# The mLSTM of a hybrid encoder block issued in one written order, its decay rows loaded and masked apart, and waits kept per tile

## The chip, the core and the metric

The kernel runs on one core of a Trainium2 chip. The core has four compute engines with their own instruction streams (TensorE, called PE in the profile; VectorE, DVE; ScalarE, ACT; GpSimd, POOL) and SyncE (SP), whose stream here only issues DMA transfers. ScalarE issues transfers too. Each engine takes its instructions strictly in the order of its stream; engines wait for one another by semaphores. The metric is the device time of one execution in microseconds (us). The kernel before took 2719.76 us in the median of three runs, 2715.68 to 2721.2.

## The reference, cut to what matters

One layer on x of 2048 positions by 1024 channels, all float32: a pre-norm, one input projection, two groups of heads side by side, an output projection with residual, and a squared-ReLU MLP with residual. Group A is four heads of a bidirectional mLSTM, in chunks of 128 positions (16 per head); group B is a Hyena long convolution by FFT. The part that the change rewrites is group A:

```python
def mlstm_chunkwise(q, k, v, log_i, log_f):          # one direction, heads of 128 channels
    bcum = jnp.cumsum(log_f.reshape(B, H, NC, L), axis=-1); g = bcum[..., -1]
    a = g[..., None] - bcum + li
    def step(carry, xs):                             # the state, from chunk to chunk
        m_new = jnp.maximum(g_c + m, jnp.max(a_c, axis=-1))
        decay = jnp.exp(g_c + m - m_new); w = jnp.exp(a_c - m_new[..., None])
        C_new = decay[..., None, None] * C + jnp.einsum('bhl,bhld,bhle->bhde', w, k_c, v_c)
        n_new = decay[..., None] * n + jnp.einsum('bhl,bhld->bhd', w, k_c)
    dmat = jnp.where(causal, bcum[..., :, None] - bcum[..., None, :] + li[..., None, :], -jnp.inf)
    m_t = jnp.maximum(bcum + m_s[..., None], jnp.max(dmat, axis=-1))
    s_qk = jnp.einsum('bhctd,bhcsd->bhcts', qc, kc) * jnp.exp(dmat - m_t[..., None])
    inter_scale = jnp.exp(bcum + m_s[..., None] - m_t)
    num = einsum(s_qk, vc) + inter_scale[..., None] * einsum(qc, C_s)
    den = s_qk.sum(-1) + inter_scale * einsum(qc, n_s)
    return num / jnp.maximum(jnp.abs(den), jnp.exp(-m_t))[..., None]
h_m = (h_fwd + h_bwd) * o_gate                       # then an RMS norm per head
```

## The kernel before, in words

The program is one stream of stages: pre-norm and input projection (with the Hyena filters beside it), the Hyena convolutions with the last pieces of the projection woven in, the mLSTM, the output projection, the MLP. All matrices stay in float32; each large product is three passes of TensorE (lines 159 to 161) over split operands.

`mlstm()` (L881) does the four heads in a software pipeline over n = 0 to 68. The names, which the rows use:

- `turned(h, g)`, L939: four transposes `ptk` of a key group into one PSUM tile `kt`, of which there is one, and from it the weighted keys `kw`, four ScalarE instructions for the forward direction (L950) and one of VectorE for the backward one (L952). Head h+1 is turned in steps 6 to 9 of head h.
- `state_step(h, step)`, L954: four products `pv` (two directions) and two VectorE updates `st` (L971) that carry the states from chunk to chunk. Head h+1's fifteen steps run two per n from step 8 of head h; head 0's fifteen all stand ahead of n = 0.
- `weights(h, g)`, L974: the load of the decay rows `mb` of four chunks, broadcast to 128 partitions, and two GpSimd masks (L980, L981).
- `scores(h, ch)`, L984: the products `pS` of a chunk, two ScalarE exponentials on `mb` (L993), and for every fourth chunk one VectorE product `pm` of scores and weights (L996).
- `values(h, ch)`, L999, five steps later: the products `ps` (query by state) and `pa` (weights by v); `scaled` (two ScalarE instructions `nm`, L1015), `sums` (VectorE, L1018), and for every fourth chunk the quotients `den` (VectorE) with `nm` times `den` and `ht` (GpSimd, L1028, L1030), stored by ScalarE's queue (`ym<-ht`). These later pieces are kept in a list and issued at the end of step n by `issue(n)`.

PSUM tiles of `pv`, `ps` and `pa` come from one pool of five (`mps`). Loads of the next heads' k, v and q stand in a table `LOADS` by step.

The order: the Hyena part runs inside `tc.manual_schedule()`, in which every engine issues what the code emits, in that order. `mlstm()` does not; there a scheduler orders the emitted work by its own estimate of when each piece is ready. Tile pools have a rule for reusing bytes of pools that were released: by default a first user waits for all users of those earlier pools; with `reuse_waits="tile"` it waits only for users of the earlier tiles on its own bytes. Three pools had that before.

Of the kernel before, what the change touches and what calls it, by code (L numbers as in the profile page):

```python
# [147 lines left out]
class Builder:  # L148
# [95 lines left out]
    def build(self):  # L244
        tc, nc = self.tc, self.nc
        with ExitStack() as c:
            cp = c.enter_context(tc.tile_pool(name="cp", bufs=1))
# [24 lines left out]
            with ExitStack() as c2:  # L272
                self.pw = pj.enter_context(tc.tile_pool(name="pwk", bufs=2, reuse_waits="tile"))
                self.pp = pj.enter_context(tc.tile_pool(name="pps", bufs=4, space=PSUM))
# [7 lines left out]
            gp = c.enter_context(tc.tile_pool(name="gp", bufs=1, side="right"))  # L282
# [6 lines left out]
            for i, n in enumerate(("mlstm_norm_w", "hyena_norm_w")):  # L289
# [3 lines left out]
                   hy.enter_context(tc.tile_pool(name="hps", bufs=3, space=PSUM, side="right")))  # L293
# [7 lines left out]
            op = self.op = late.enter_context(tc.tile_pool(name="opre", bufs=1, side="right"))  # L301
# [3 lines left out]
            self.mtail = late.enter_context(tc.tile_pool(name="mtail", bufs=2, side="right"))  # L305
# [5 lines left out]
            self.h1p = c.enter_context(tc.tile_pool(name="h1p", bufs=2, space=PSUM))  # L311
            oc = ExitStack()
            self.hq = c.enter_context(tc.tile_pool(name="hmq", bufs=1))
# [6 lines left out]
            hp = c.enter_context(tc.tile_pool(name="hmp", bufs=1, side="right"))  # L320
            self.hm_pool.update({i: hp for i in (1, 2)})
            self.hm = {}
            self.cb = c.enter_context(tc.tile_pool(name="cb", bufs=1, side="right"))
# [10 lines left out]
    def long_conv(self, pools, hy, early):  # L334
# [16 lines left out]
    def filters(self, c, consts):  # L351
        tc = self.tc
        kp = c.enter_context(tc.tile_pool(name="kp", bufs=1, side="right"))
        wk = c.enter_context(tc.tile_pool(name="kwk", bufs=2, side="right"))
        ps = c.enter_context(tc.tile_pool(name="kps", bufs=2, space=PSUM, side="right"))
        yield from self.filter_net(kp, wk, ps, consts)
        yield from self.filter_spectra(kp, wk, ps, c.enter_context(tc.tile_pool(name="kmps", bufs=1, space=PSUM, side="right")))
# [523 lines left out]
    def mlstm(self):  # L881
# [3 lines left out]
        for ready in range(AHEAD // 4):  # L885
            self.weights(0, ready)
# [1065 lines left out]
```

## Time and profile before

| | us |
|---|---|
| median of three runs (2715.68 to 2721.2) | 2719.76 |
| the profiled execution | 2723.08 |
| its span, first to last instruction | 2721.3 |
| TensorE busy in it | 2602.7 (96%) |
| last projection piece to the first value step `ps` | 1026.4 to 1046.4 |
| value steps of head 0, 1, 2, 3 begin (n = 5, 16, 32, 48 of the pipeline) | 1046.4, 1069.1, 1107.2, 1144.1 |
| last `pa` of the mLSTM | 1174.1 |

The profile is one execution; times inside it are from its first instruction. Busy time is the union of an engine's instructions; the matmuls' ends are modelled, so the start of the next matmul says more of what one costs than its own length. The time in brackets behind a row is how long the engine stood idle before it, and after the arrow what ended that. "Granted clock" is the share of TensorE's full clock that the chip gave in that stretch; its two levels are 1.2 and 2.4 GHz.

### The profile page before, as it was taken

How to read it: one execution, taken by the hardware profiler on the slowest of the kernel's cores; microseconds unless marked ns; L12 is line 12 of the kernel's file. 1: busy time of each engine (PE TensorE's matmuls, PEld its weight loads, DVE VectorE, ACT ScalarE, POOL GpSimd, SP SyncE). 2: the span in 40 equal slices, each digit the busy share in tenths (PEclk: the TensorE clock that was granted, in tenths of full speed). 3: DMA queues.
4: the chain of work that ended last, by engine and by line, in shares of the span. 5: the costliest groups of instructions: out<-in, count | busy, mean ns of one | idle time of the engine just before them, and what ended most of it. 6: DMA issues, size and time to landing. Idle time of an engine off the chain costs nothing.

```text
span 2721.3 us, 35529 instructions
## 1 busy us (share of the span) xinstructions
PE 2602.7 (96%) x12293; PEld 2125.3 (78%) x12293; DVE 1527.1 (56%) x2453; ACT 1237.2 (45%) x2300; POOL 1220.3 (45%) x973
## 2 busy tenths in 40 slices
PE   6999999999999998889997999989999999999998
PEld 4778888777798887767775888868888888888876
DVE  5676653777547666656455444464444433544478
ACT  6355544555544446643334454454444333222244
POOL 1211114555235443446676877677772340311232
PEclk8999999999999999989998999989999999999999
DMA  6233346665676549556755444554446453444546
GB/s 172 61 87 113 112 124 215 191 190 175 215 234 185 181 154 297 152 158 222 231 177 200 171 138 166 181 185 150 148 163 254 164 181 108 121 146 159 186 161 218
DMA packets 288355, 465.76 MB, mean 171 GB/s; under 512 B 37542, under 2 KB 149414, under 8 KB 287152
## 3 DMA queue, kind: packets, MB, share of 16 engines
q1 hardware_dynamic: 227600, 324.85, 38.3%
q10 hardware_dynamic: 53264, 117.53, 11.4%
q0 software_dynamic: 7312, 21.11, 3.1%
q8 instruction: 98, 1.61, 0.3%
q14 instruction: 81, 0.66, 0.1%
HBM read 289.27 MB, written 174.13 MB: 170 GB/s over the span
## 4 chain that ended last, share of the span: by engine, by line
PE 40%; DVE 5%; POOL 3%; DMA 3%; ACT 2%; issue 2%; ACTq 0%; DVEq 0%; POOLq 0%; SPq 0%
PE pm L160 13%; PE pm L161 13%; PE pm L159 13%; DVE cb L169 1%; POOL xt L1255 1%; DVE hm L169 1%; ACT xo L1393 1%; DMA m<-ga 1%; DVE hm L1877 0%; DMA m<-in_w_mlp_out_dram 0%; POOL cb L169 0%; DMA hm<-ht 0%; DVE xo L1396 0%; POOL ht L1428 0%; DVE hm L1807 0%
## 5 line engine op out<-in xcount | busy, mean ns | idle before, releaser
L166 ACT CAST cb<-m 128x1024 fp32r<-128x1024 f32 (+1 forms) x346 | 281.2, 847 | 442.6 <-PE pm L159 387.5
L169 DVE TENSOR_TENSOR cb<-m,cb 128x1024 fp32r<-128x1024 f32 (+1 forms) x222 | 232.5, 1084 | 306.0 <-ACT cb L166 296.3
L160 PE MATMUL pm<-hm,cb 128*128 128x512 f32 x896 | 354.6, 396 | 18.4 <-DVE hm L169 13.2
L159 PE MATMUL pm<-hm,cb 128*128 128x512 f32 x896 | 354.1, 396 | 11.1 <-POOL cb L169 6.2
L161 PE MATMUL pm<-hm,cb 128*128 128x512 f32 x896 | 352.8, 394 | 0.0
L160 PE MATMUL pm<-cb 128*128 128x512 f32 x880 | 343.4, 390 | 7.8 <-DVE cb L169 7.8
L159 PE MATMUL pm<-cb 128*128 128x512 f32 x880 | 342.3, 389 | 1.0 <-DVE cb L169 1.0
L161 PE MATMUL pm<-cb 128*128 128x512 f32 x880 | 342.5, 389 | 0.0
L169 POOL TENSOR_TENSOR cb<-m,cb 128x1024 fp32r<-128x1024 f32 x124 | 270.7, 2196 | 71.6 <-ACT cb L166 71.6
L1689 DVE TENSOR_TENSOR m<-pm,m 128x512 f32<-128x512 f32 x224 | 154.2, 690 | 250.8 <-PE pm L161 224.7
L159 PE MATMUL pt<-hn,w 128*128 128x512 f32 x640 | 270.1, 422 | 1.7 <-ACT hn L486 1.6
L160 PE MATMUL pt<-hn,w 128*128 128x512 f32 x640 | 254.2, 397 | 0.3 <-DVE hn L487 0.2
L161 PE MATMUL pt<-hn,w 128*128 128x512 f32 x640 | 253.3, 396 | 0.0
L169 POOL TENSOR_TENSOR raw<-raw,hi 128x512 fp32r<-128x512 f32 x160 | 206.1, 1300 | 100.6 <-ACT hi L166 75.4
L160 PEld LDWEIGHTS pm<-hm,cb 128*128 128x128 f32 x896 | 170.5, 190 | 59.3 <-DVE hm L169 16.6
L159 PEld LDWEIGHTS pm<-hm,cb 128*128 128x128 f32 x896 | 170.6, 190 | 51.0 <-POOL cb L169 7.9
L160 PEld LDWEIGHTS pm<-cb 128*128 128x128 f32 x880 | 165.1, 188 | 45.9 <-DVE cb L169 11.8
L161 PEld LDWEIGHTS pm<-hm,cb 128*128 128x128 f32 x896 | 170.4, 190 | 36.1
L159 PEld LDWEIGHTS pm<-cb 128*128 128x128 f32 x880 | 165.1, 188 | 35.9 <-ACT junk L1862 1.4
L161 PEld LDWEIGHTS pm<-cb 128*128 128x128 f32 x880 | 165.2, 188 | 34.0
L1693 ACT ACTIVATE m<-m 128x512 f32<-128x512 f32 x128 | 80.5, 630 | 220.4 <-DVE m L1689 213.1
L635 POOL DMA_DIRECT2D vp<-vst x96 | 61.3, 642 | 232.0 <-ACT vst L631 230.9
(322 smaller groups left out, 5672.0 us busy)
## 6 DMA issues: line engine op xcount, KB each, us to landing
ga<-m ACTq DMA_DIRECT2D x96, 512.0 KB, 4.4
m<-ga SPq DMA_DIRECT2D x96, 512.0 KB, 3.8
d<-st ACTq DMA_DIRECT2D x64, 512.0 KB, 3.0
m<-in_w_mlp_in_dram SPq DMA_DIRECT2D x62, 512.0 KB
m<-in_w_mlp_out_dram SPq DMA_DIRECT2D x114, 256.0 KB, 4.0
raw<-d SPq DMA_DIRECT2D x96, 256.0 KB, 3.2
xt<-in_x_dram SPq DMA_DIRECT2D x32, 512.0 KB, 4.0
dk<-kst SPq DMA_DIRECT2D x32, 512.0 KB, 3.8
```

Of the source, the lines that this page charges most:

```text
L159: pe.matmul(ps, w[1], x[0], start=first, stop=False)
L160: pe.matmul(ps, w[0], x[1], start=False, stop=False)
L161: pe.matmul(ps, w[0], x[0], start=False, stop=last)
L166: self.act.copy(hi, src)
L169: (eng_lo or self.dve).tensor_tensor(lo, src, hi.bitcast(F32), ALU.subtract)
L635: pool.dma_start(dst[:, 8 * b + e:8 * b + 8:2, cc:cc + 128], st[64 * e:64 * e + 64])
L1255: eng.tensor_tensor(res[:, cs], tmp[e], res[:, cs], ALU.add)
L1393: act.activation(x1, xt, AF.Square, accum_out=ss1[:, h:h + 1])
L1689: dve.tensor_tensor(dst, a, b, ALU.add)
L1693: act.activation(g, g, AF.Relu)
```

## The change

1. Nearly all tile pools get `reuse_waits="tile"`.
2. `mlstm()` runs inside `tc.manual_schedule()`.
3. `weights` is cut in two: `weights_load` (the transfer) and `masked` (the two GpSimd masks), issued at different steps.
4. Head 0's fifteen state steps are spread over n = 0 to 4, three each.
5. `issue(n)` stands at the start of step n; `scaled` is emitted with `values` itself; `pm` is put off to the start of the next step.
6. `LOADS` begins with head 1's k at n = 1 (before: ahead of n = 0); head 1's v and q follow at 3 and 6; the rest is unchanged. The loads for the output projection (`loads_ahead`) go at n = 30 to 48, every second step, where they went at 50 to 59.
7. Head 0's weighted-key tiles are allocated before its k, v and q (`weighted_keys`), and the Hyena part allocates its first `st` and `ci` tiles first, which decides whose places the mLSTM's first tiles take.
8. The projection's last column group is stored by ScalarE's queue, no longer SyncE's (eight transfers `vo<-vst`).

The diff, cut to its core (the other pools change as the first one shown):

```diff
-            cp = c.enter_context(tc.tile_pool(name="cp", bufs=1))
+            cp = c.enter_context(tc.tile_pool(name="cp", bufs=1, reuse_waits="tile"))
...
-            self.mps = ms.enter_context(tc.tile_pool(name="mps", bufs=5, space=PSUM))
-            self.mlstm()
+            self.mps = ms.enter_context(tc.tile_pool(name="mps", bufs=5, space=PSUM, reuse_waits="tile"))
+            with tc.manual_schedule():
+                self.mlstm()
...
+        self.kw_first = {g: self.weighted_keys() for g in (0, 3, 1, 2)}
         self.head_loads(0, "kvq")
...
-                self.load(self.vo[128 * t - 128:128 * t + 128, N * g:N * g + n].rearrange("(u p) c -> p u c", p=128),
+                (self.store if g == order[-1] else self.load)(self.vo[128 * t - 128:128 * t + 128, N * g:N * g + n].rearrange("(u p) c -> p u c", p=128),
                           sts.pop((g, t // 2))[:, :, 0:n])
...
-        LAG, AHEAD = 5, 10
-        LOADS = {1: "v1", 5: "q1", 9: "k2", 14: "v2", 19: "q2", 32: "k3", 32 + LAG: "v3", 40: "q3"}
+        LAG = 5
+        LOADS = {1: "k1", 3: "v1", 6: "q1", 9: "k2", 14: "v2", 19: "q2", 32: "k3", 32 + LAG: "v3", 40: "q3"}
         self.later = []
-        for ready in range(AHEAD // 4):
-            self.weights(0, ready)
-        ready += 1
-        self.head_loads(1, "k")
-        for step in range(15):
-            self.state_step(0, step)
+        for g in range(4):
+            self.weights_load(0, g)
+        for g in range(2):
+            self.masked(0, g)
         for n in range(64 + LAG):
             self.now = n
             h, ch = divmod(n, 16)
-            while ready < 16 and ready <= (n + AHEAD) // 4:
-                self.weights(*divmod(ready, 4))
-                ready += 1
+            if n % 4 == 1 and 4 <= n // 4 + 3 < 16:
+                self.weights_load(*divmod(n // 4 + 3, 4))
+            self.issue(n)
             steps = [s for s in (2 * ch - 16, 2 * ch - 15) if h < 3 and 0 <= s < 15]
+            if n < 5:
+                for s in range(3 * n, 3 * n + 2):
+                    self.state_step(0, s)
+            if steps:
+                self.state_step(h + 1, steps[0])
             if n < 64:
-                if steps:
-                    self.state_step(h + 1, steps[0])
                 self.scores(h, ch)
                 if h < 3 and 6 <= ch < 10:
                     self.turned(h + 1, (0, 3, 1, 2)[ch - 6])
             if LAG <= n:
                 self.values(*divmod(n - LAG, 16))
+            if n < 5:
+                self.state_step(0, 3 * n + 2)
             if len(steps) > 1:
                 self.state_step(h + 1, steps[1])
             if n in LOADS:
                 self.head_loads(int(LOADS[n][1]), LOADS[n][0])
-            if 50 <= n < 60:
-                self.loads_ahead(n - 50)
+            if n % 4 == 3 and n // 4 + 2 < 16:
+                self.masked(*divmod(n // 4 + 2, 4))
+            if 30 <= n < 50 and n % 2 == 0:
+                self.loads_ahead((n - 30) // 2)
             if n in (61, 64, 64 + LAG - 1):
                 self.first_gate((61, 64, 64 + LAG - 1).index(n))
-            self.issue(n)
...
+    def weighted_keys(self):
+        return [self.mearly.tile([128, 4, 128], F32, tag=f"kw{d}", name=f"kw{d}", bufs=4) for d in range(2)]
...
-        if i == 3:
+        def weighted():
             pm = m["pm", g] = wk.tile([128, 2, 4, 128], F32, tag="pm", name="pm")
             self.dve.scalar_tensor_tensor(pm, pS.unsqueeze(1).to_broadcast([128, 2, 4, 128]), KSCALE, mb,
                                           ALU.mult, ALU.mult)
+        if i == 3:
+            self.later.append((self.now + 1, weighted))
...
-        work = [scaled, sums] + ([last, None, stored] if i == 3 else [])
+        scaled()
+        work = [None, sums] + ([last, None, stored] if i == 3 else [])
```

Outside of the mLSTM and the first pieces of the output projection the engines' orders stay as they were, but for those eight stores.

What stands on VectorE at the hand-over from the Hyena part (its last rows `z`) to the mLSTM, before and then now:

```order
L1155 TENSOR_TENSOR z<-z,pu 128x512
L952 TENSOR_TENSOR kw_10341<-ptk,qt 128x512
L952 TENSOR_TENSOR kw_10353<-ptk,qt 128x512
L971 SCALAR_TENSOR_TENSOR st<-st,decay,pv 128x129 x3
L952 TENSOR_TENSOR kw_10365<-ptk,qt 128x512
L971 SCALAR_TENSOR_TENSOR st<-st,decay,pv 128x129 x5
L952 TENSOR_TENSOR kw_10377<-ptk,qt 128x512
L971 SCALAR_TENSOR_TENSOR st<-st,decay,pv 128x129 x22
L996 SCALAR_TENSOR_TENSOR pm<-pS,mb 128x1024
```

```order
L1174 TENSOR_TENSOR z<-z,pu 128x512
L960 TENSOR_TENSOR kw_10287<-ptk,qt 128x512
L960 TENSOR_TENSOR kw_10289<-ptk,qt 128x512
L960 TENSOR_TENSOR kw_10291<-ptk,qt 128x512
L960 TENSOR_TENSOR kw_10293<-ptk,qt 128x512
L979 SCALAR_TENSOR_TENSOR st<-st,decay,pv 128x129 x24
L1007 SCALAR_TENSOR_TENSOR pm<-pS,mb 128x1024
L979 SCALAR_TENSOR_TENSOR st<-st,decay,pv 128x129 x6
```

The first eight state updates stood between the weighted keys; now all thirty stand behind the fourth, and the first `pm` has moved ahead of the last six.

What stands on ScalarE in the steps of head 0 and 1 without state work, exponentials `mb` and scaled numerators `nm`, before and now:

```order
L993 ACTIVATE mb<-mb,qt 128x128
L1015 ACTIVATE nm<-ps,qt 128x129 x2
L993 ACTIVATE mb<-mb,qt 128x128 x5
L1015 ACTIVATE nm<-ps,qt 128x129 x2
L993 ACTIVATE mb<-mb,qt 128x128 x6
L1015 ACTIVATE nm<-ps,qt 128x129 x2
```

```order
L1029 ACTIVATE nm<-ps,qt 128x129 x2
L1004 ACTIVATE mb<-mb,qt 128x128 x2
L1029 ACTIVATE nm<-ps,qt 128x129 x2
L1004 ACTIVATE mb<-mb,qt 128x128 x2
L1029 ACTIVATE nm<-ps,qt 128x129 x2
L234 DMA ym<-ht 128x4x128
L1004 ACTIVATE mb<-mb,qt 128x128 x2
L1029 ACTIVATE nm<-ps,qt 128x129 x2
```

Batches of up to six exponentials stood between two steps' numerators; now it is two and two throughout, with the store in its written place.

What stands on ScalarE at the end of the mLSTM, where the output projection's weights (`wo`) and its first operand (`y`, cast from PSUM `pty`) begin, before and now:

```order
L1015 ACTIVATE nm<-ps,qt 128x129 x6
L234 DMA ym<-ht 128x4x128
L1015 ACTIVATE nm<-ps,qt 128x129 x2
L1342 ACTIVATE wo_11960<-wf_10390,yw 128x1024
L166 CAST y_10396<-pty 128x512
```

```order
L1029 ACTIVATE nm<-ps,qt 128x129 x6
L1363 ACTIVATE wo_11963<-wf_10390,yw 128x1024
L234 DMA ym<-ht 128x4x128
L1029 ACTIVATE nm<-ps,qt 128x129 x2
L166 CAST y_10396<-pty 128x512
```

The first `wo` has moved ahead of the store and of the last numerators.

## Rows read from the trace of the kernel before

**Rows 1.** The page, busy time of TensorE: us, share of the span, instructions.

```profile
PE 2602.7 (96%) x12293; PEld 2125.3 (78%) x12293; DVE 1527.1 (56%) x2453; ACT 1237.2 (45%) x2300; POOL 1220.3 (45%) x973
```

**Rows 2.** The mLSTM cut into its stages (windows): start and end, length, then busy us (and instructions) of PE, PEld, DVE, ACT and POOL, the granted TensorE clock as a share of full speed, the DMA share and GB/s.

```profile
1026.40:1046.40 20.00, 14.46 (x97) 13.24 (x97) 10.82 (x35) 11.91 (x38) 3.73 (x7) 0.83 1.07 338
1046.40:1069.10 22.70, 21.04 (x156) 19.55 (x157) 18.90 (x53) 18.44 (x67) 6.60 (x8) 1.00 0.90 300
1069.10:1107.20 38.10, 31.41 (x213) 28.85 (x212) 24.97 (x67) 25.06 (x89) 19.09 (x21) 0.91 0.77 252
1107.20:1144.10 36.90, 30.85 (x205) 28.48 (x205) 22.73 (x66) 22.82 (x79) 16.10 (x19) 0.90 0.53 143
1144.10:1174.10 30.00, 27.07 (x158) 22.38 (x156) 18.92 (x46) 16.61 (x53) 18.62 (x14) 0.94 0.22 62
```

**Rows 3.** The timeline of TensorE inside the mLSTM, two places where nothing is waited for: start us, us from the first start to the last modelled end, line, operation, output from inputs, how many. What one piece costs the engine is the start of the next minus its own.

```profile
1038.08 0.39 PE L990 MATMUL pS<-q,k 128*128 128x128 f32 x2
1038.30 0.39 PE L966 MATMUL pv<-v,kw 128*128 128x129 f32 x2
1038.52 0.61 PE L990 MATMUL pS<-q,k 128*128 128x128 f32 x4
...
1048.02 0.60 PE L1008 MATMUL ps<-st,q 128*128 128x258 f32 x2
1048.46 0.61 PE L1010 MATMUL pa<-v,pm 128*128 128x129 f32 x4
1048.90 0.60 PE L945 MATMUL ptk<-eye,k 128*128 128x128 f32 x4
1049.34 0.60 PE L1008 MATMUL ps<-st,q 128*128 128x258 f32 x2
```

**Rows 4.** The hand-over from the Hyena part to the mLSTM, the timeline of SyncE's queue (one row) and of TensorE (three rows): the same columns, and in brackets the idle time before and what ended it.

```profile
1022.85 0.33 SPq L231 DMA_DIRECT2D k<-qk  x1
...
1027.87 0.63 PE L945 MATMUL ptk<-eye,k 128*128 128x128 f32 x4 [1.46 <-DMA k<-qk]
1030.57 1.12 PE L945 MATMUL ptk<-eye,k 128*128 128x128 f32 x4 [2.06 <-DVE kw L952]
...
1046.43 0.67 PE L1008 MATMUL ps<-st,q 128*128 128x258 f32 x2 [1.60 <-DVE st L971]
```

**Rows 5.** Groups of the stretch 1020 to 1195, ScalarE first and VectorE behind: count | busy us, mean ns of one | idle us before them and what ended it.

```profile
L993 ACT ACTIVATE mb<-mb,qt 128x128 f32<-128x128 f32 x128 | 42.4, 406 | 12.3 <-POOL mb L980 5.6 <-POOL ht L1030 3.6 <-DVE st L971 3.0
L1015 ACT ACTIVATE nm<-ps,qt 128x129 f32<-128x129 f32 x128 | 39.8, 373 | 33.4 <-PE ps L1008 17.0 <-POOL ht L1030 14.8 <-PE pa L1010 1.2
...
L971 DVE SCALAR_TENSOR_TENSOR st<-st,decay,pv 128x129 f32<-128x129 f32 x120 | 34.0, 342 | 13.3 <-PE pv L966 13.1
L1018 DVE TENSOR_TENSOR nm<-nm,pa 128x258 f32<-128x258 f32 x64 | 26.4, 419 | 25.4 <-ACT nm L1015 22.1 <-PE pS L990 2.2 <-PE pa L1010 0.2
L996 DVE SCALAR_TENSOR_TENSOR pm<-pS,mb 128x1024 f32<-128x1024 f32 x16 | 19.5, 1218 | 4.3 <-PE pa L1010 3.6 <-PE pS L990 0.5
```

**Rows 6.** Timelines, runs of one kind of instruction without a wait between them: ScalarE's exponentials (its window ends at 1042, so six of them), ScalarE's scaled numerators, VectorE's state updates.

```profile
1040.51 1.86 ACT L993 ACTIVATE mb<-mb,qt 128x128 f32<-128x128 f32 x6
...
1171.76 1.64 ACT L1015 ACTIVATE nm<-ps,qt 128x129 f32<-128x129 f32 x6
...
1040.50 5.78 DVE L971 SCALAR_TENSOR_TENSOR st<-st,decay,pv 128x129 f32<-128x129 f32 x22 [0.58 <-PE pv L966]
```

**Rows 7.** The timeline of TensorE, the first three transposed key groups of head 2 (they run during head 1).

```profile
1077.79 0.60 PE L945 MATMUL ptk<-eye,k 128*128 128x128 f32 x4
...
1082.39 0.60 PE L945 MATMUL ptk<-eye,k 128*128 128x128 f32 x4
...
1088.53 1.06 PE L945 MATMUL ptk<-eye,k 128*128 128x128 f32 x4
```

**Rows 8.** The v of head 3: its load on SyncE's queue, and the first state product that reads it on TensorE.

```profile
1112.40 0.36 SPq L231 DMA_DIRECT2D v<-vo  x1
...
1121.48 0.77 PE L966 MATMUL pv<-v,kw 128*128 128x129 f32 x2 [3.80 <-DMA v<-vo]
```

**Rows 9.** The way into the output projection, the timelines of TensorE (two rows) and ScalarE (three rows), and VectorE's group of weight products of the stretch 1020 to 1195. py are the Hyena gate's last products, a group of TensorE in 1144.1 to 1174.1.

```profile
1178.97 1.02 PE L159 MATMUL po<-wo,y 128*128 128x512 f32 x2 [3.02 <-DVE y L169]
...
1192.24 0.50 PE L159 MATMUL po<-wo,yt 128*128 128x512 f32 x1 [3.23 <-DVE yt L169]
...
1175.45 0.40 ACTq L234 DMA_DIRECT2D ym<-ht  x1
1175.90 0.63 ACT L1015 ACTIVATE nm<-ps,qt 128x129 f32<-128x129 f32 x2 [2.50 <-POOL ht L1030]
1176.41 1.15 ACT L1342 ACTIVATE wo<-wf,yw 128x1024 fp32r<-128x1024 f32 x1
...
L1343 DVE SCALAR_TENSOR_TENSOR wo<-wf,yw,wo 128x1024 fp32r<-128x1024 f32 x4 | 6.5, 1636 | 0.0
...
L1290 PE MATMUL py<-rd,s1i 128*128 128x512 f32 x4 | 1.9, 592 | 0.0
```

**Rows 10.** The first weights of the MLP: two rows of SyncE's queue, and GpSimd's instruction before them.

```profile
1419.03 0.54 SPq L231 DMA_DIRECT2D xt<-in_x_dram  x1
1422.46 0.93 SPq L231 DMA_DIRECT2D m<-in_w_mlp_in_dram  x2
...
1421.16 1.27 POOL L169 TENSOR_TENSOR cb<-wr,cb 128x512 fp32r<-128x512 f32 x1
```

More of the change, by code (lines that the diff above doesn't have):

```diff
@@ L273, in build @@
                 self.pw = pj.enter_context(tc.tile_pool(name="pwk", bufs=2, reuse_waits="tile"))
-                self.pp = pj.enter_context(tc.tile_pool(name="pps", bufs=4, space=PSUM))
+                self.pp = pj.enter_context(tc.tile_pool(name="pps", bufs=4, space=PSUM, reuse_waits="tile"))
                 work = self.project()
@@ L281, in build @@
             self.gates_done = False
-            gp = c.enter_context(tc.tile_pool(name="gp", bufs=1, side="right"))
+            gp = c.enter_context(tc.tile_pool(name="gp", bufs=1, side="right", reuse_waits="tile"))
             self.qt = gp.tile([128, 4, 128], F32, name="qt")
@@ L292, in build @@
             hyp = (hy.enter_context(tc.tile_pool(name="hwk", bufs=2, side="right", reuse_waits="tile")),
-                   hy.enter_context(tc.tile_pool(name="hps", bufs=3, space=PSUM, side="right")))
+                   hy.enter_context(tc.tile_pool(name="hps", bufs=3, space=PSUM, side="right", reuse_waits="tile")))
             with tc.manual_schedule():
@@ L299, in build @@
             hs.close()
-            op = self.op = late.enter_context(tc.tile_pool(name="opre", bufs=1, side="right"))
+            op = self.op = late.enter_context(tc.tile_pool(name="opre", bufs=1, side="right", reuse_waits="tile"))
             self.ahead = {k: op.tile([128, D], F32, name=f"wf{k}") for k in range(4, 8)}
@@ L492, in normalise @@
         act, dve = self.act, self.dve
-        wk = c.enter_context(tc.tile_pool(name="nwk", bufs=2))
-        ps = c.enter_context(tc.tile_pool(name="nps", bufs=3, space=PSUM, side="right"))
+        wk = c.enter_context(tc.tile_pool(name="nwk", bufs=2, reuse_waits="tile"))
+        ps = c.enter_context(tc.tile_pool(name="nps", bufs=3, space=PSUM, side="right", reuse_waits="tile"))
         xs = {}
@@ L945, in turned @@
             self.pe.transpose(pt[:, i, :], m["k"][:, cc:cc + 128], self.eye)
-        kw = [wk.tile([128, 4, 128], F32, tag=f"kw{d}", name=f"kw{d}", bufs=4) for d in range(2)]
-        m["kw", g] = kw
+        kw = m["kw", g] = self.kw_first.pop(g) if h == 0 else self.weighted_keys()
         c0 = 16 * h + 4 * g
@@ L1095, in first @@
             self.store(dst, st)
+        ahead = {"st": pair(), "ci": wk.tile([128, 128], F32, tag="ci", name="ci", bufs=3)}
         s1 = constant("c_s1")
@@ L1189, in hyena @@
                 if j < 31 or j == 31:
-                    ci[j] = wk.tile([128, 128], F32, tag="ci", name="ci", bufs=3)
+                    ci[j] = ahead.pop("ci", None)
+                    if ci[j] is None:
+                        ci[j] = wk.tile([128, 128], F32, tag="ci", name="ci", bufs=3)
                     self.load(ci[j], io["c_s2i"][j])
@@ L1452, in out_proj @@
         staged = self.first_operands(scratch)
-        wl = c.enter_context(tc.tile_pool(name="owl", bufs=2, side="right"))
+        wl = c.enter_context(tc.tile_pool(name="owl", bufs=2, side="right", reuse_waits="tile"))
         for i in range(18):
```

46 lines of the change are left out of this document (25 added, 21 removed).

## The prediction, made before the changed kernel was run

> **What bounds the kernel now.** I read the page first: TensorE is busy 2602.7 us, 96% of the span [rows 1], so all that a change of order can win is in some 119 us of idle TensorE and in stretches at a lower clock. Windows along the span show that the only stretch that the change reorders, the mLSTM, is the poorest: by stages [rows 2] the hand-over has 14.46 of 20.0 us busy, the steps of heads 1 and 2 have 31.41 of 38.1 and 30.85 of 36.9, and the granted clock is 0.83, 0.91 and 0.90 there against 1.00 in the rest of head 0. Next, the timeline of TensorE gives the price of a step where nothing waits [rows 3]: two `pS` start 0.22 us before the next piece, two `ps` 0.44, four `pa` 0.44, four `ptk` 0.44, and two `pv` 0.22, so 0.44 for a state step. A step without state work is 0.22+0.44+0.44 = 1.10; one with two state steps 1.98; a whole head 16x1.10 + 15x0.44 + 4x0.44 = 26.0. Heads 1 and 2 take 38.1 and 36.9. What ends the waits is read from the groups [rows 5]: ScalarE's `nm` sits behind GpSimd's `ht` for 14.8 us and its exponentials for 3.6, because a store that waits for `ht` stands ahead of them in its queue; VectorE's sums wait 22.1 us for `nm`. So the mLSTM is bound by a loop over engines, TensorE to ScalarE to VectorE and back through five PSUM tiles, not by one engine.
>
> **The change part by part.** The sum is made against the profiled execution, 2723.1 us, and carried over to the median of the runs, 2719.8, as a difference.
>
> *Hand-over and first steps.* Head 0's k went out on SyncE's queue at 1022.85 and TensorE waited 1.46 us for it [rows 4]. The narrower waits and the first places let the load go before the last Hyena stores, so I count the 1.46 as gone. Late next is the single `kt` tile: one transposed group to the next took 1030.57-1027.87 = 2.70 us [rows 4], through four `kw` of ScalarE and one of VectorE. Four groups from 1026.4 on end at 1026.4+4x2.7 = 1037.2. VectorE now holds all thirty `st` behind the fourth `kw`; before, eight were done by then. At 5.78/22 = 0.263 each [rows 6] and one `pm` of 1.22 [rows 5] between, that is 30x0.263+1.22 = 9.1, so the first `ps` comes at 1046.3 at best; if TensorE stays at the lower clock during the state steps, two or three later. Before it came at 1046.43 [rows 4]. I take **+1.5**, bounds -0.1 and +2.3: the 1.46 that the load gives is paid back by VectorE.
>
> *Turned steps.* In the written order TensorE cannot pass a `ptk` whose `kt` is not free, so steps 6 to 9 of a head take the 2.70 of the loop, the last somewhat more (3.1, an estimate with one `ps` in its way): 3x2.7+3.1 = 11.2.
>
> *State steps, n = 10 to 15 of a head.* TensorE needs 1.98; VectorE four `st`, one sum of 0.42 and a quarter of a `pm`, 1.05+0.42+0.30 = 1.77 [rows 5, 6] and the small quotients besides. I take 2.1, since each waits a little for the other; 6x2.1 = 12.6.
>
> *Other steps.* ScalarE's two exponentials and two `nm` cost 2x0.31+2x0.273 = 1.17 [rows 6], and its store of 0.40 [rows 9] in every fourth; I take 1.25, against TensorE's 1.10. The wait for `ht` was (14.8+3.6)/16 = 1.15 a group before [rows 5]. The store keeps its distance to `ht` in steps, while `pm` and the issue list move by one; I take 1.0 for each group where no state work hides it.
>
> By stage, against [rows 2]:
> - rest of head 0, eleven steps: 1.25+11.2+12.6 = 25.05 against 22.70, **+2.3**. Before, the scheduler let other work run between the transposes here; now it cannot.
> - head 1: 6x1.25+1.0+11.2+12.6 = 32.3 against 38.1, **-5.8**.
> - head 2: the same and the wait for v of head 3. That load goes out at 1112.40 and its reader started at 1121.48 [rows 8], 9.1 us later; in the new order load and reader keep their steps, 37 and 40, which leave some 3x2.7 = 8 us or less, so 0 to 2.4; I take 1.2: 33.5 against 36.9, **-3.4**.
> - head 3 and the tail: 16x1.25+4x1.0, five last steps at 0.9 (an estimate: `ps` and `pa` are 0.88), and the gate's six `py` at 1.9/4 each [rows 9], 2.9: 31.4 against 30.0, **+1.4**.
> - the clock: all this stands at full clock. If heads 1 and 2 keep the 0.90 that they had, a fifth of the time runs at half speed, and a step costs 2.20 or 3.96 there: 0.2x(0.95+1.86)x6 = 3.4 a head. The waits that the order now makes are about 1.1 us (2.70 less TensorE's 1.54), shorter than the one of 3.80 [rows 8]. So I choose 1.0 a head, nearer to nothing: **+2.0**.
>
> What the row shows of the clock is 1.00 in the stage with the fewest pauses and 0.90 in those with more [rows 2]. The Trainium skill (TensorE: Matmul & The Clock Gate, section "A second HAM failure mode: psum-queue depth-cycling") says that a kernel which walks through PSUM banks pauses so often between groups of matmuls that the clock swings between its levels. By that rule the written order, which adds a short pause to each turned step, would lose the whole 3.4 a head or more; the trace agrees that the clock falls here, but not yet that short pauses do it.
>
> *Into the output projection.* TensorE waits 3.02 for `y` and 3.23 for `yt` [rows 9]. ScalarE's first `wo` (1.15, at 1176.41) now runs in the 2.50 us in which the store waited, so `y` is about 1.0 earlier. Against it the last group's quotients stand on VectorE between `wo` products of 1.64 [rows 9], so its `ht` and what is loaded back from it come some 4 us later, which gives most back at the next operand. **-0.2**, bounds -2.6 and +2.0.
>
> *The MLP's first weights* went out at 1422.46, just after GpSimd's row of 1421.16+1.27 [rows 10]; with waits by tile that wait goes, and SyncE's queue is free from 1419.03+0.54. Up to 2.9 us earlier, but VectorE's own chain into the MLP stays as it was: **-0.5**, bounds -2.9 and 0.
>
> *At nothing*: the stores moved to ScalarE's queue (eight at 0.4), the pools of the first 1000 us, and the Hyena order. TensorE covers them, busy in nine tenths of the span [rows 1]; without that cover the stores would cost 3.2. The loads ahead for the output projection go out earlier, into a DMA share of 0.53 [rows 2]; nothing waits for them before.
>
> Sum: 1.5+2.3-5.8-3.4+1.4+2.0-0.2-0.5 = **-2.7**: 2720.4 for the profiled execution, **2717.1** for the median.
>
> **The rivals.**
> - *More: every step at TensorE's own price* but for the `kt` loop. Then a head is 11.2+6x1.10+6x1.98 = 29.7, so -8.4 and -7.2 for heads 1 and 2; the rest of head 0 is 24.2, +1.5; head 3 and tail 16x1.10+5x0.88+2.9 = 24.9, -5.1; with -0.7 behind and no loss in the ramp -19.9: **2700**. For it: ScalarE's price of 1.17 is within 0.07 of TensorE's. Against it: `ht` still stands ahead of `nm` in a queue that has an order.
> - *Slower: the `kt` loop in company.* During head 1 the turned groups came 4.6 and 6.1 us apart [rows 7], not 2.70, since ScalarE's exponentials and VectorE's `st` stand between `ptk` and `kw`. If the loop keeps 4.6, each of twelve turned steps costs 1.9 more and TensorE, now held at the `ptk`, cannot fill it: +22.8, so +20.1: **2740**. It decides from about 3.4 on, where the sum turns slower by over 5.4. Against it: the written order puts a step's `kw` right behind its exponentials.
> - *No gain: the clock stays at 0.90* in heads 1 and 2, +6.8 in place of 2.0: +2.1, **2722**; at the 0.83 of the hand-over [rows 2] a third of the time is at half speed, 5.7 a head, and with head 0's state steps (3.8) +15.2 in place of 2.0: **2730**. This is the result by the rule that the page states.
> - *Only the waits act*: the new order equals the scheduler's, and what remains is the load's 1.46 and the MLP's: -2 to -4, which the forecast's own range holds.
>
> **How the numbers follow.** A measurement tells from no change what is over 0.2%, 5.4 us: 2714.3 to 2725.2 is "the same". The forecast with its own range of 2711 to 2723 gets 0.45 (of it 0.15 faster, 0.28 same, 0.02 slower), the rival "more" 0.25 (faster), the `kt` loop 0.13 (0.11 slower, 0.02 same), the clock 0.17 (0.08 same, 0.09 slower). So faster 0.40, same 0.38, slower 0.22. The range reaches toward 2700 on the one side and takes in the clock's first step on the other: 2702 to 2727.
>
> **What would show it.** Right: the first `ptk` directly behind the last projection piece, near 1026.4, and the first `ps` at 1047 to 1049; `ptk` groups 2.7 to 3.1 apart in all heads; head 1 and head 2 at 32 to 35 us between their first `ps`; rest of head 0 longer than 22.7; single waits of over 2 us gone in heads 1 and 2 except at v of head 3. Wrong: `ptk` groups over 3.4 apart, a clock under 0.90 in heads 1 and 2, or a first `ps` after 1050; and on the other side heads under 30 us.

## The result, and the profile after

The changed kernel took 2727.24 us in the median (six runs, 2723.52 to 2728.79) against 2717.57 for the kernel before: ratio 1.0034, 95% interval 1.0021 to 1.0046. Run again beside later experiments it took 2725.82, ratio 1.0027 (1.0015 to 1.0038). So the change makes the kernel 6 to 10 us slower, where 2717.1 and a small gain were forecast.

Single profiles of one kernel scatter by two or three us: the changed kernel's 200th matmul started at 68.48 in one profile and at 65.36 in the other. Stages are therefore read from profiles, totals from the runs, and a stage of one profile is good to about two us: the hand-over in the order of the changed kernel took 22.92 and 24.78 us in its two profiles, and 22.9 to 25.0 in the four experiments below that leave it as it is. The stages below are counted in the traces between starts of matmuls, in us; "waits only" is an experiment told below, with the order of before.

| stage | before | forecast | after | after, again | waits only |
|---|---|---|---|---|---|
| last projection piece to first `ps` | 20.30 | 21.8 | 22.92 | 24.78 | 19.50 |
| rest of head 0 | 22.69 | 25.05 | 24.82 | 24.25 | 22.49 |
| head 1 | 38.06 | 32.3 | 32.09 | 32.68 | 35.93 |
| head 2 | 36.93 | 33.5 | 38.18 | 38.89 | 37.03 |
| head 3 to the last `pa` | 29.71 | 31.1 | 31.31 | 31.33 | 29.65 |
| to the first product with `y` | 5.16 | | 5.56 | 5.52 | 5.17 |
| to the first product with `yt` | 13.27 | | 14.20 | 14.20 | 13.32 |
| to the 6000th matmul | 33.80 | | 34.60 | 34.52 | 33.77 |
| sum | 199.91 | 197.7 | 203.68 | 206.17 | 196.86 |

The forecast's column is before with each term of the forecast on it; its sum takes in the 2.0 for the clock and the -0.2 into the output projection, and is 199.91 less 2.2, the -2.7 of the forecast without the -0.5 at the MLP. The same stages as windows of the changed kernel, with the way to the first `yt` as a sixth row; columns as in [rows 2]:

```profile
1027.10:1050.00 22.90, 13.12 (x91) 12.15 (x90) 11.73 (x35) 9.85 (x30) 5.53 (x13) 0.85 0.72 220
1050.00:1074.80 24.80, 23.44 (x164) 21.89 (x165) 17.54 (x53) 16.59 (x58) 6.53 (x6) 0.93 0.51 172
1074.80:1106.90 32.10, 28.18 (x206) 25.61 (x206) 23.18 (x67) 22.86 (x81) 17.07 (x20) 1.00 0.55 167
1106.90:1145.10 38.20, 30.53 (x206) 28.02 (x205) 23.38 (x67) 22.88 (x81) 17.03 (x20) 0.87 0.85 292
1145.10:1176.70 31.60, 27.89 (x168) 21.48 (x167) 18.57 (x44) 23.49 (x77) 18.07 (x17) 1.00 0.26 74
1176.70:1196.20 19.50, 9.54 (x33) 6.58 (x31) 16.24 (x17) 9.72 (x14) 9.66 (x5) 0.78 0.50 163
```

Head 1 is what the written order can do: 32.1 us at full clock. Head 2 has the same instructions and takes 6.1 more. Its DMA share is 0.85, where [rows 2] had 0.53, and its clock is down to 0.87. In the second profile the hand-over ran at a lower clock than here, 0.72, and head 1 at 0.95, 0.6 us longer:

```profile
1022.60:1047.40 24.80, 15.66 (x91) 14.72 (x90) 11.94 (x35) 9.86 (x30) 5.54 (x13) 0.72 0.72 199
...
1071.70:1104.30 32.60, 29.53 (x205) 26.89 (x205) 23.07 (x67) 22.82 (x81) 16.98 (x20) 0.95 0.51 161
```

The hand-over, timelines of TensorE, ScalarE and VectorE of the changed kernel, answering to [rows 4] and [rows 6]:

```profile
1027.22 0.60 PE L954 MATMUL ptk<-eye,k 128*128 128x128 f32 x4
1031.64 1.12 PE L954 MATMUL ptk<-eye,k 128*128 128x128 f32 x4 [3.82 <-DVE kw L960]
...
1050.02 0.67 PE L1022 MATMUL ps<-st,q 128*128 128x258 f32 x2 [2.66 <-DVE st L979]
...
1029.72 1.14 ACT L958 ACTIVATE kw<-ptk,qt 128x128 f32<-128x128 f32 x4 [1.91 <-DMA d<-st]
...
1040.22 0.69 DVE L960 TENSOR_TENSOR kw<-ptk,qt 128x512 f32<-128x512 f32 x1 [2.42 <-ACT kw L958]
1040.83 6.36 DVE L979 SCALAR_TENSOR_TENSOR st<-st,decay,pv 128x129 f32<-128x129 f32 x24
1047.10 1.23 DVE L1007 SCALAR_TENSOR_TENSOR pm<-pS,mb 128x1024 f32<-128x1024 f32 x1
1048.23 1.64 DVE L979 SCALAR_TENSOR_TENSOR st<-st,decay,pv 128x129 f32<-128x129 f32 x6
```

The wait for k is gone: the transposes stand right behind the projection. But ScalarE's first weighted key then waits 1.91 us for the landing of the Hyena part's store `d<-st`. Behind it VectorE's chain runs without a gap: 24 `st`, the `pm`, six `st`, and then the first `ps`. In the second profile the same wait is 2.20 and its row names a load of decay rows (`mb<-mrow`); by the trace's landing times the store's last part came in at 1025.42 there and the key began at 1025.52, so the store fits it as well. In the kernel before, ScalarE's first and VectorE's fourth weighted key:

```profile
1028.59 1.14 ACT L950 ACTIVATE kw<-ptk,qt 128x128 f32<-128x128 f32 x4 [1.75 <-PE ptk L945]
...
1039.23 0.69 DVE L952 TENSOR_TENSOR kw<-ptk,qt 128x512 f32<-128x512 f32 x1 [0.88 <-ACT kw L950]
```

The last projection piece started at 1026.13 there and at 1027.10 in the changed kernel. So VectorE's fourth key began 13.10 us behind it before and 13.12 now: the wait for k that went bought nothing.

Turned groups of head 2 in the changed kernel, TensorE's timeline, answering to [rows 7]:

```profile
1082.10 0.60 PE L954 MATMUL ptk<-eye,k 128*128 128x128 f32 x4
1086.58 0.66 PE L954 MATMUL ptk<-eye,k 128*128 128x128 f32 x4 [2.49 <-DVE kw L960]
1089.74 0.60 PE L954 MATMUL ptk<-eye,k 128*128 128x128 f32 x4
1092.30 0.66 PE L954 MATMUL ptk<-eye,k 128*128 128x128 f32 x4
```

They are 4.48, 3.16 and 2.56 apart, with one real wait, at the first pair.

The v of head 3 in the changed kernel, SyncE's queue and TensorE, answering to [rows 8]:

```profile
1106.02 0.34 SPq L231 DMA_DIRECT2D k<-qk  x1
1106.39 0.43 SPq L231 DMA_DIRECT2D wf<-in_w_out_dram  x1
1107.94 0.37 SPq L231 DMA_DIRECT2D mb<-mrow  x1
1108.36 0.97 SPq L231 DMA_DIRECT2D wf<-in_w_out_dram  x2
1113.20 0.38 SPq L231 DMA_DIRECT2D mb<-mrow  x1
1113.68 0.55 SPq L231 DMA_DIRECT2D v<-vo  x1
...
1125.08 1.20 PE L974 MATMUL pv<-v,kw 128*128 128x129 f32 x4 [4.60 <-DMA v<-vo]
```

Three of the output projection's weight loads (`wf`, 0.5 MB each) now stand ahead of v. It goes out at 1113.68 and its reader starts at 1125.08, 11.4 us later; before it was 9.1. TensorE came to the reader 6.8 us behind the issue. In the second profile it waited 5.87.

In the kernel before, the scheduler had sent the same loads much earlier than their place in the code, steps 50 to 59, suggests. The first and the last of the eight `wf` and `wfa` on SyncE's queue:

```profile
1062.85 1.73 SPq L231 DMA_DIRECT2D wf<-in_w_out_dram  x1
...
1096.37 0.43 SPq L231 DMA_DIRECT2D wfa<-in_w_out_dram  x1
```

All of them were out before the v of head 3 at 1112.40 [rows 8], and so was head 3's k, at 1096.00 (1106.02 in the changed kernel). So the written order moved these loads later, not earlier, and into v's way.

The end of the mLSTM in the changed kernel, timelines of TensorE, ScalarE, VectorE and GpSimd, answering to [rows 9]:

```profile
1181.97 0.80 PE L159 MATMUL po<-wo,y 128*128 128x512 f32 x1 [4.84 <-DVE y L169]
...
1196.17 0.79 PE L159 MATMUL po<-wo,yt 128*128 128x512 f32 x1 [4.89 <-DVE yt L169]
...
1180.09 0.63 ACT L1029 ACTIVATE nm<-ps,qt 128x129 f32<-128x129 f32 x2 [3.35 <-POOL ht L1044]
1180.61 0.58 ACT L166 CAST y<-pty 128x512 fp32r<-128x512 f32 x1
...
1193.05 1.15 ACT L1363 ACTIVATE wo<-wfa,yw 128x1024 fp32r<-128x1024 f32 x1 [4.91 <-POOL ht L1044]
1194.11 0.57 ACT L166 CAST yt<-ptp 128x512 fp32r<-128x512 f32 x1
...
1173.81 0.20 DVE L241 RECIPROCAL gr_r<-gr_sd 128x8 f32<-128x8 f32 x1 [0.93 <-ACT gr_sd L239]
1173.93 0.37 DVE L1032 TENSOR_TENSOR nm<-nm,pa 128x258 f32<-128x258 f32 x1
1174.33 0.82 DVE L1038 SCALAR_TENSOR_TENSOR den<-nm,qt 128x8 f32<-128x8 f32 x1
...
1177.34 1.31 DVE L1364 SCALAR_TENSOR_TENSOR wo<-wf,yw,wo 128x1024 fp32r<-128x1024 f32 x1
...
1177.65 1.95 POOL L1044 TENSOR_TENSOR ht<-nm 128x512 f32<-128x512 f32 x1
```

ScalarE casts `y` and `yt` behind instructions that stood 3.35 and 4.91 us behind a store waiting for `ht`. The first of these `ht` is late because the group's sums and quotients stand on VectorE behind `gr_r`, a reciprocal of the Hyena gate, which waits for ScalarE. In the kernel before, the quotients stood ahead of it:

```profile
1171.13 0.20 DVE L1026 RECIPROCAL den<-den 128x8 f32<-128x8 f32 x1
1171.88 0.20 DVE L241 RECIPROCAL gr_r<-gr_sd 128x8 f32<-128x8 f32 x1 [0.55 <-ACT gr_sd L239]
```

The second `ht` (1190.54) stands on GpSimd behind the gate's `yz` (1188.56); before, it stood ahead of it (1179.74 and 1184.90). In the order of before ScalarE's wait at the first place was 2.50 [rows 9]. This is read from the timelines; no run moves these two pieces alone.

### The profile page after: what moved, and what is told of

Read it like the earlier page. It is cut to its first block, busy times and chain, and to the rows that moved or that the text cites. A ratio compares the mean times of both kernels' runs of the same rounds, so it can differ in the third digit from the quotient of the medians.

```text
span 2723.7 us, 35490 instructions
## 1 busy us (share of the span) xinstructions
PE 2599.7 (95%) x12293; PEld 2122.4 (78%) x12293; DVE 1531.3 (56%) x2453; ACT 1237.6 (45%) x2300; POOL 1220.7 (45%) x973
## 3 DMA queue, kind: packets, MB, share of 16 engines
q10 hardware_dynamic: 55440, 119.66, 11.5%
## 4 chain that ended last, share of the span: by engine, by line
PE 39%; DVE 4%; POOL 4%; DMA 3%; ACT 2%; issue 2%; ACTq 0%; SPq 0%; DVEq 0%; POOLq 0%
PE pm L160 13%; PE pm L161 13%; PE pm L159 13%; DMA hm<-ht 1%; POOL xt L1276 1%; DVE cb L169 1%; POOL cb L169 1%; DMA m<-in_w_mlp_out_dram 1%; ACT xo L1414 1%; DVE hm L169 1%; DVE hm L1898 0%; DVE xo L1417 0%; DMA m<-in_w_mlp_in_dram 0%; ACTq L234 0%; DVE gss L1318 0%
```

## The experiments

Twelve kernels, one of them the changed kernel again, each timed in five rounds beside the kernel before on the same chip. Two chips were used, so distances to the changed kernel are taken from the ratios to the kernel before. Two theories stood at first. A: the written order costs the time, at places named above. B: the narrower waits cost it, since transfers start into each other.

**Waits by tile alone.** In the kernel before, 26 pools changed as this one (six pools, not three, had the rule already):

```diff
-            self.mps = ms.enter_context(tc.tile_pool(name="mps", bufs=5, space=PSUM))
+            self.mps = ms.enter_context(tc.tile_pool(name="mps", bufs=5, space=PSUM, reuse_waits="tile"))
```

> The kernel before with one part of the change alone: waits by tile in all those pools; every engine's order is that of before. Theory A (the written order of the mLSTM costs the time: hand-over, head 0, the wait for v of head 3, the end): within 0.1% of before, 2715 to 2720. Theory B (the narrower waits cost it, since transfers start into each other): 4 to 8 us over before, and the stretches outside of the mLSTM longer.

2716.81 us, ratio 0.9992 (0.9983 to 1.0001): a gain of some 2 us, at the edge of what can be told. B falls.

**The order alone.** The changed kernel with those 26 pools put back.

> The changed kernel with the pools' waits as before; every engine's order is that of the changed kernel. Theory A: as slow as the changed kernel or 1 to 2 us slower (head 0's k is waited for again), 8 to 12 us over before. Theory B: within 3 us of before.

2725.62 us, ratio 1.0027 (1.0016 to 1.0038). The loss comes with the order. The two runs also split the profile. From the 6800th to the 8400th matmul, the MLP's first third, the two kernels without waits by tile took 411.1 and 411.5 us, and of the twelve profiles with them eleven took 407.4 to 409.5 (one 412.4).

**Weight loads late.**

```diff
-            if 30 <= n < 50 and n % 2 == 0:
-                self.loads_ahead((n - 30) // 2)
+            if 50 <= n < 60:
+                self.loads_ahead(n - 50)
```

> The changed kernel with the loads for the output projection back at steps 50 to 59. Theory A with the cause that those loads stand ahead of head 3's v in the queue and share its bandwidth: TensorE's wait for v falls from 4.60 us to under 2, head 2 from 38.2 us to 34 to 35, and the whole is 3 to 4 us under the changed kernel. Rival (v's own megabyte takes that long, or the reader simply comes earlier): the wait stays at 4 to 5 us and the time at that of the changed kernel.

2723.03 us, ratio 1.0017 (1.0009 to 1.0026), 3 to 4 us under the changed kernel. The wait shrank only to 3.43, and head 2 to 35.92. SyncE's queue and TensorE:

```profile
1116.23 0.41 SPq L231 DMA_DIRECT2D v<-vo  x1
...
1126.09 1.20 PE L974 MATMUL pv<-v,kw 128*128 128x129 f32 x4 [3.43 <-DMA v<-vo]
```

Without the weight loads v still took 9.9 us from issue to reader, against 9.1 in the kernel before. So most of the wait is that v is asked for too late; the loads add the rest. Both theories of this run were half right.

**Head 3's v ahead.**

```diff
-        LOADS = {1: "k1", 3: "v1", 6: "q1", 9: "k2", 14: "v2", 19: "q2", 32: "k3", 32 + LAG: "v3", 40: "q3"}
+        LOADS = {1: "k1", 3: "v1", 6: "q1", 9: "k2", 14: "v2", 19: "q2", 26: "v3", 32: "k3", 40: "q3"}
...
-            v = m["v"] = wk.tile([128, 16, 129], F32, tag="v", name="v")
+            v = m["v"] = wk.tile([128, 16, 129], F32, tag="v", name="v", bufs=3 if h else 1)
```

> The changed kernel with a third buffer for v and head 3's v loaded at step 26, not 37. Theory A (the wait for v of 4.6 us is a real loss on the path): the wait is gone, head 2 takes 33 to 34 us in place of 38.2, and the whole is 4 to 5 us under the changed kernel, 2722 to 2723. Rival (another wait takes its place: the turned groups behind the one `kt` tile, or the exponentials): head 2 stays over 36 and the gain is under 2 us.

2717.51 us, ratio 0.9996 (0.9987 to 1.0005): 8 to 10 us under the changed kernel, more than was expected and more than the stages show, 4.0 against its first profile and 6.5 against its second. Head 2 takes 31.98 in its profile, 6.2 less than in the changed kernel, and the state product that waited 4.60 for v waits 0.85 for its keys, although the weight loads stand where the change put them. That product and head 2's window in that run, columns as in [rows 2]:

```profile
1121.31 0.49 PE L974 MATMUL pv<-v,kw 128*128 128x129 f32 x2 [0.85 <-DVE kw L960]
...
1107.10:1139.10 32.00, 28.07 (x207) 25.61 (x206) 23.19 (x67) 22.91 (x81) 16.97 (x19) 1.00 0.95 313
```

The clock is back at 1.00, at a DMA share of 0.95. So it was not the traffic that had taken the clock down: the lower clock went with the long wait, and the two made 6.2 out of 4.6.

**The end to the scheduler.** The written order up to step 60 only:

```diff
-            with tc.manual_schedule():
-                self.mlstm()
+            self.mlstm()
...
+            if n == 0:
+                hold = ExitStack()
+                hold.enter_context(self.tc.manual_schedule())
+            if n == 61:
+                hold.close()
```

> The changed kernel with the written order up to step 60 of the mLSTM only; the last eight steps go to the scheduler again. Theory A (the end loses because the last groups' quotients and their stores stand behind the gate's and the weights' instructions): TensorE's waits for the first y and the first yt fall from 4.84 and 4.89 us to 3.0 to 3.5, and the whole is 2 to 4 us under the changed kernel. Rival (the end is late because the mLSTM before it is): waits and time stay within 1 us.

2717.22 us, ratio 0.9993 (0.9984 to 1.0002). TensorE's rows:

```profile
1177.43 0.50 PE L159 MATMUL po<-wo,y 128*128 128x512 f32 x1 [2.37 <-DVE y L169]
...
1188.95 0.80 PE L159 MATMUL po<-wo,yt 128*128 128x512 f32 x1 [3.33 <-DVE yt L169]
```

The waits were 4.84 and 4.89; in the kernel before they were 3.02 and 3.23 [rows 9]. Head 3 takes 28.25 to its last `pa` in place of 31.31, and the way from the last projection piece to the 6800th matmul is 6.7 us shorter than in the changed kernel's first profile (9.3 than in its second). The runs gain 9 to 11. The gain is larger than expected: the written order cost not only the two waits but 3 us in the last steps of head 3 as well.

**The last stores on SyncE's queue.**

```diff
-            self.store(self.ym[:, 128 * h:128 * h + 128].rearrange("(c p) d -> p c d", p=128)[:, 4 * g:4 * g + 4], m["hs"])
+            (self.load if h == 3 and g > 1 else self.store)(self.ym[:, 128 * h:128 * h + 128].rearrange("(c p) d -> p c d", p=128)[:, 4 * g:4 * g + 4], m["hs"])
```

> The changed kernel with the last two stores of the mLSTM's output (`ym<-ht`, head 3's third and fourth group) issued by SyncE's queue, not ScalarE's. Theory A (at the end ScalarE stands in its queue behind a store that waits for GpSimd's `ht`, 3.35 and 4.91 us): TensorE's waits of 4.84 for `y` and 4.89 for `yt` fall to 1.5 to 3 each, and the whole is 3 to 5 us under the changed kernel. Rival (VectorE's order is the cause: quotients behind the gate's reduction and between the weight products): the waits fall by under 1 us and the time stays within 1 us of the changed kernel.

2724.2 us, ratio 1.0016 (1.0007 to 1.0025), 3 to 5 us under the changed kernel by the ratios, 2 to 3 by the medians. TensorE's rows:

```profile
1181.42 0.50 PE L159 MATMUL po<-wo,y 128*128 128x512 f32 x1 [3.35 <-DVE y L169]
...
1192.02 0.71 PE L159 MATMUL po<-wo,yt 128*128 128x512 f32 x1 [1.40 <-DVE yt L169]
...
1202.44 1.11 PE L1327 MATMUL ptp<-eye,ymt 128*128 128x128 f32 x4 [3.01 <-POOL ymt L1321]
```

The waits fall by 1.5 and 3.5, and 3.01 come back ten us later: the stored rows are read back as `ymt`, and `ht` itself is as late as it was. So ScalarE's queue passes the lateness on; that VectorE's order makes it is the reading of the timelines above. Which of the two decides the time is not settled by this run; that the last eight steps' order does is shown by the run before it.

**First places as before.** The lines on `kw_first` and on the Hyena's first tiles taken out.

> The changed kernel with the mLSTM's first tiles allocated as before (k, v, q first, weighted keys later; no Hyena tiles allocated first). In the changed kernel the first weighted key starts 2.6 us behind the last projection piece, 1.9 us after its transposes are done. Theory A: that wait is for the place (the Hyena stores' landing), so it goes, and the first `ps` comes 1.5 to 2 us earlier than in the changed kernel; the whole 1 to 2 us under it, 2725 to 2726. Rival (the places do nothing): all as in the changed kernel.

2720.67 us, ratio 1.0008 (0.9999 to 1.0018). ScalarE's row:

```profile
1027.66 1.14 ACT L957 ACTIVATE kw<-ptk,qt 128x128 f32<-128x128 f32 x4 [0.58 <-PE ptk L953]
```

The wait for `d<-st` is gone and the first `ps` comes 21.9 us behind the projection, 1.0 less than in the changed kernel's first profile and 2.9 less than in its second. The runs show 5 to 7 us of gain, the stages 1.0 against the first profile and 3.5 against the second; what the rest is stays open.

**Both ends to the scheduler.** As the run on the end, from step 5 on only.

> The changed kernel with the written order in steps 5 to 60 of the mLSTM only: head 0's state steps (n = 0 to 4) and the last eight steps go to the scheduler. The hand-over took 20.3 us from the last projection piece to the first `ps` in the kernel before and 22.9 in the changed one. Theory A (VectorE's order costs it: eight state updates moved behind the fourth weighted key, 8 x 0.263 = 2.1 us, and a `pm` of 1.22 ahead of the last six): back to 20 to 20.5, and 2 to 3 us under the run with only the end freed, 2714 to 2716. Rival (the weighted keys' places, whose last writers' stores land late, set it): 22 to 23 us stay, and the time stays at 2717.

2716.06 us, ratio 0.9989 (0.9981 to 0.9998), 1.2 under the run on the end, which the scatter hardly resolves. VectorE's rows:

```profile
1038.57 0.69 DVE L964 TENSOR_TENSOR kw<-ptk,qt 128x512 f32<-128x512 f32 x1 [0.88 <-ACT kw L962]
1039.84 4.23 DVE L983 SCALAR_TENSOR_TENSOR st<-st,decay,pv 128x129 f32<-128x129 f32 x16 [0.58 <-PE pv L978]
1043.99 1.22 DVE L1011 SCALAR_TENSOR_TENSOR pm<-pS,mb 128x1024 f32<-128x1024 f32 x1
1045.12 1.63 DVE L983 SCALAR_TENSOR_TENSOR st<-st,decay,pv 128x129 f32<-128x129 f32 x6
```

The eight updates are early again and the `pm` is not; the first `ps` comes at 21.7, half way between the theory and the rival.

**All three mended.** Both ends to the scheduler, first places as before, v ahead.

> The changed kernel with three terms of the loss undone together: the scheduler for steps 0 to 4 and from 61 on, the first places as before, and a third v buffer with head 3's v loaded at step 26. Theory A (the terms are separate and add up: ends -6 to -8, v -6, places -1 from the profiles): 12 to 15 us under the changed kernel run beside it, 2708 to 2711. Rival (they are one chain, each hides the next): no lower than the best of them alone, 2715 to 2718.

2709.49 us, ratio 0.9966 (0.9954 to 0.9979): 16 us under the changed kernel beside it and 10 under the kernel before. By stages, against the profile of the changed kernel from the same round, the two ends are worth 9.0, the first places 3.5 and v 6.5, together 19.0; all three together are worth 15.7. The difference lies in the hand-over, where two of the mends hide each other: 21.71 us with the first steps free, 21.88 with the first places back, 21.78 with both. With both, ScalarE's first key comes early, but VectorE's first one is released by `d<-st` (at 1028.89) and TensorE then waits 1.18 for v. The other terms add up. The gains of the single runs, 10 to 12, 5 to 7 and 8 to 10 us by the ratios, add up to more than the 17 to 18 that all three have by the same measure; why is not shown. It is the fastest of the study, together with the next one.

**The written order from step 16 on.**

> As the run before it, with the written order from step 16 on only, so that all of head 0 goes to the scheduler. Theory A (the written order costs the rest of head 0 about 2 us, since TensorE is held at the single transpose tile, and gains in heads 1 and 2): 1.5 to 2.5 us under the run before it, head 0's rest 22 to 23 us in place of 24 to 25. Rival: the hand-over between the two ways in the middle of the pipeline costs as much as it saves; the same time.

2709.64 us, ratio 0.9966 (0.9955 to 0.9978): the same time. Head 0's rest is 21.43 against 24.24 in its profile, but head 1 starts mixed, 33.59 against 32.71. Up to the 6000th matmul the stages are 3.1 us shorter; in the same profile the stretch from the 6800th to the 8400th took 412.4 us against 409.5, which gives 2.9 back. Whether that is chance one profile cannot tell. Inconclusive.

**The scheduler with v ahead.** The kernel before with waits by tile, the third v buffer and head 3's v at step 26.

> The kernel before with waits by tile and with the third v buffer and head 3's v at step 26: the scheduler's order throughout. The written order's gain in head 1 was 38.1 to 32.1 us, but 35.9 with the waits alone. Theory A (in heads 1 and 2 the written order itself is faster): heads 1 and 2 stay at 35 to 36 and 33 to 35 us, 2712 to 2715. Rival (what holds the scheduler's heads is v and the transfers only): both fall to 32 to 33, and the whole to 2706 to 2709.

2714.6 us, ratio 0.9983 (0.9973 to 0.9992). Heads 1 and 2 take 36.71 and 35.63, where the written order has 32.71 and 31.99 (all three mended). So in those heads the written order itself is worth 3.6 to 4.0 us each.

**The changed kernel again.**

> The changed kernel once more, beside the next three on one chip, since its six runs (2723.5 to 2728.8) lie higher above the kernel before than its profile does: from the last projection piece to the MLP (the 6800th matmul) it takes 383.0 us against 378.9. If the loss is what the stages show, 4 to 6 us over before: 2722 to 2725. If some 5 us of it lie elsewhere, 2726 to 2729 again.

2725.82 us, as told at the top: 6.3 over before, and its stages show the same: their sum of 206.17 is 6.3 over the 199.91 of before. The 9.7 of the first six runs (2727.24 less 2717.57) is 3 to 6 us more than the stages of the two profiles show; where that lies is open.

## Why the prediction was wrong

The stages without a late transfer came out as worked, one of them in part by luck. The waits did not: three terms of the sum were too small, and together they turned the sign. Against the changed kernel's first profile:

- *Head 1*, forecast 32.3: 32.09 and 32.68. *Rest of head 0*, 25.05: 24.82. *Head 3*, 31.1 to the last `pa`: 31.31. That head 1 agrees to 0.2 is the luck. By the starts of its `ps` the four turned steps took 12.9 where 11.2 was forecast, the six state steps 11.5 (12.6), and the other six 7.7 (7.5 and 1.0 for a wait). The spacing of the transposes, 2.7 to 3.1, was 2.6 to 4.5 there.
- *Head 2*, forecast -3.4, was +1.25. The failed step is "0 to 2.4; I take 1.2" with "nothing waits for them before": v's landing was compared with 8 us from issue to reader, and the reader came after 6.8; and the weight loads, costed at nothing, went into the same queue just ahead of v. Their premise, "go out earlier, into a DMA share of 0.53", was read from the steps in the code; in the trace of before they are out by 1096.4, and the written order sends them from 1106.4 on, beside a DMA share of 0.85. 4.60 of wait and the clock behind it, 6.2 in all where 1.2 stood. 4.65 of the 6.0 us by which the stages miss are here.
- *Hand-over*, forecast +1.5 with an upper end of 2.3, was +2.6. "I count the 1.46 as gone" failed: the wait for k went, and the first weighted key, given the Hyena stores' place, waited 1.91 instead. It started 2.62 us behind the projection's last piece; before, 1028.59 less 1026.13, 2.46. "4x2.7" failed with it: ScalarE's keys came 3.1 apart, and VectorE began its `st` 13.7 behind the projection (1040.83 less 1027.10) where 10.8 was counted. What VectorE adds from there was as counted: 9.1, measured 9.2 (to 1050.02). Against the kernel before that is 8 x 0.263 and 1.22, less 0.66 of gaps that closed, 2.66. In the second profile the hand-over was +4.5, at a clock of 0.72 in place of 0.85: the "two or three later" that the forecast named for a low clock came on top.
- *Into the output projection*, forecast -0.2 with an upper end of +2.0, was +2.1: 0.40, 0.93 and 0.80 in the three stages. The failed step is "so `y` is about 1.0 earlier": it took the 2.50 wait for `ht` as fixed, and the written order moved `ht` itself, by the gate's reciprocal ahead of the sums.
- *The clock*, +2.0 in heads 1 and 2 for the short pause that each turned step was to add. Those pauses did not come: head 1 has three of 0.4 us or more (2.49, 0.85 and 0.40). It ran at 1.00 in the first profile and at 0.95 in the second, 0.6 us longer; head 2 fell to 0.87 after the one long wait. By the rule of the Trainium skill that was weighed (TensorE: Matmul & The Clock Gate, "A second HAM failure mode: psum-queue depth-cycling") the whole 3.4 a head would have gone; the trace does not show that, and with so few pauses it does not test the rule either.
- *The MLP's start*, -0.5 with a lower end of -2.9: the first weights now go out right behind `xt` (1424.75 behind 1424.11), where [rows 10] had 3.4 us between them, and the two kernels with and without waits by tile differ by two us or so in the MLP's first third. *At nothing* held for the stores on ScalarE's queue as far as the profiles tell; it did not hold for the loads ahead.

The misses, 4.65 + 1.1 + 2.3 less the 2.0 of the clock, are 6.05, and 203.68 less 197.7 is 6.0. In the second profile the stages miss by 8.5, 3.0 of it at the hand-over and 5.4 in head 2, where the wait for v is longer. The forecast's own signs of being wrong came too: `ptk` groups over 3.4 apart (4.48), a clock under 0.90 in head 2 (0.87) and a first `ps` after 1050 (1050.02). The rivals did not describe it: of `kt` in company only the first pair of a head came, 4.48 apart, the clock of head 2 went with the wait for v, and none had a late transfer as its place. Of the 9.7 us of the first six runs, 3 to 6 stay without a place.

## What to carry to other kernels

A written order and a scheduler are not one choice: here the order was worth some 4 us a head in the steady part and lost it at both ends, where another stage's work mixes in, so each stretch is to be priced apart. Before transfers are moved "at nothing", read from the trace, not from the code, when the scheduler had sent them; then look at what follows them in the queue and how many us lie between its issue and its reader. A wait that is removed at a load can come back at the first tile on the place that the load's neighbour left.

## What the runs showed of the hardware that was not expected

The Hyena part's last store `d<-st` landed 3.0 us after its issue in the kernel before (1019.89, and k, which waited for it, went out at 1022.85), and 8.9 us after it in the changed kernel (1020.85, and the weighted key that waited began at 1029.72). Between lies that k, v and q, 3 MB, went out at 1015 to 1016, ahead of the store. The landing times in all fourteen profiles bear this out: 8.5 to 9.2 us in the twelve in which k had gone out ahead of the store, and 2.8 and 2.9 us in the two in which k went out behind it (the kernel before, and the order alone). How the loads slow it is not shown.

GpSimd's `ht` takes 1.09 us alone and 1.95 beside VectorE's `wo`. In the run with the stores on SyncE's queue the two met in the other order, GpSimd first:

```profile
1178.59 1.09 POOL L1044 TENSOR_TENSOR ht<-nm 128x512 f32<-128x512 f32 x1
...
1178.61 2.16 DVE L1364 SCALAR_TENSOR_TENSOR wo<-wf,yw,wo 128x1024 fp32r<-128x1024 f32 x1 [0.25 <-ACT wo L1363]
```

There `ht` took its 1.09 and the `wo`, 1.31 in the changed kernel, took 2.16: in these two cases the one that started first ran at its own price, and the other took 0.85 more. The Trainium skill (SBUF — State Buffer, section "SBUF: two separate sides") says so of a VectorE instruction with two SBUF inputs against a GpSimd one that reads SBUF; the trace agrees.
